# Attention scores from stacked high and low parts: two matmuls over 128 rows in place of three over 64

## The chip, the cores and the metric

The kernel runs on one core of a Trainium2 chip. The metric is the device time of one execution in microseconds (us). Times are given as the median of several executions. One further execution was recorded by the hardware profiler; every duration of a single instruction below comes from it. TensorE is called PE in the profile, VectorE is DVE, ScalarE is ACT, GpSimd is POOL and SyncE is SP.

## What is computed

One layer of a decoder on 512 tokens of width 1024: a SwiGLU feed-forward layer (FFN 1), a mixer, and a second feed-forward layer (FFN 2), each with an RMS norm before and after. The mixer projects the tokens to a pooling part and to an attention part. The attention part has 8 query heads and 2 key/value heads of 64 elements, looks back over 128 tokens and works in blocks of 128 queries. Of the reference, this is what the change touches:

```python
def swa_with_sinks(q, k, v, sinks):
    ...
    kb = jnp.concatenate([kp[:, :-1], kp[:, 1:]], axis=2)
    vb = jnp.concatenate([vp[:, :-1], vp[:, 1:]], axis=2)
    s = jnp.einsum('bnqkgd,bnjkd->bnkgqj', qb, kb,
                   preferred_element_type=jnp.float32) * (HEAD_DIM ** -0.5)
    ...
    s = jnp.where(valid[None, :, None, None], s, NEG_INF)
    ...
    p = jax.nn.softmax(jnp.concatenate([s, sink], axis=-1), axis=-1)[..., :-1]
    o = jnp.einsum('bnkgqj,bnjkd->bnqkgd', p.astype(v.dtype), vb)
    return o.reshape(B, S, ATTN_WIDTH)
```

## The kernel before

All products are made from split numbers. A float32 operand is written as a high part (a cast to the type fp32r, made by ACT) and a low part (the operand less its high part, made by DVE or POOL), and `mm3` (lines 363 to 368) adds three matmuls: high by high, high by low, low by high. In the profile the three are lines L366, L367 and L368.

The work comes in three stages. `gate_up` and `down_proj` do FFN 1 up to about 350 us of the span. The mixer runs between about 350 and 490 us. FFN 2 fills the rest. The mixer is not a stage of its own in the code: `gate_up("f2", ...)` calls `last_steps` ahead of its first block, and that calls `mixer()` and `output()`. Since `gate_up` makes its first four blocks inside `in_order()` (line 521), the instructions of PE, DVE, ACT and POOL in all of the mixer stand on their engines in the order in which the code writes them.

`mixer()` (lines 1169 to 1260) is that order, written out by hand. The four token tiles t = 0 to 3 (128 tokens each) pass through these steps, which are interleaved with one another and with the pooling part:

- `qkv_block(t)` projects the tile to q, k and v on PE; `qkv_out(t)` copies the result to the tile `z` (ACT, L966 to L971) and rotates a part of it (POOL, L977 to L981).
- `turn(t)` transposes k (one transpose, bank `tk`) and q (four, bank `tq`) on PE (L988, L990), so that the 64 elements of head group v lie on partitions 64v to 64v+63. Then ACT copies the high part of k (L991) and of q (L994) out of the banks, each over all 128 partitions at once, and DVE subtracts (L992, L995) for the low parts.
- `scores(t)` makes the scores of the 8 heads, in four PSUM banks of two heads. A head takes the three matmuls of `mm3` on the 64 partitions of its group; the stationary operand is q (64x128), the moving one is k: 256 keys, or 128 for t = 0. That makes 24 matmuls for a tile.
- `tops(t)` adds the mask to the scores and takes the maxima (DVE, L1025), then makes the negated maximum `nm` (L1033) and `es` (L1035). `exps(t, half)` takes the exponentials on ACT (L1041, L1046), four heads in each half. `normalise(t)` divides: the sum on DVE (L1052, L1053), four heads on DVE (L1056) and four on ACT (L1058).
- `turn_probs(t, v)` transposes the probabilities on PE (L1067, bank `pt`) and splits them on ACT (L1071, `ph`) and DVE (L1072, `pl`). `values(t, v)` multiplies them by v on PE and copies the result on ACT (L1083, `o`).
- `pool_in`, `pool_sums`, `pool_mid` and `pool_out` are the pooling part. Its projection (tile `pu`) is the PE work that `run(g)` puts between the attention steps; its sums run on POOL. `pool_out` reads its bank `py` twice on ACT (L1150, L1152) and once on DVE (L1153).
- `W.more(n)` splits n weight tiles ahead of their use: the high part on ACT (L166); the low part (L172) on POOL within `qkv_block` 2 and 3, on DVE elsewhere.

PSUM has 8 banks in one pool. The 24 tiles of 128x512 in the pool `h` are shared by keys, queries, probabilities and the rest; a tile takes a slot at its first write and gives it back after its last reader.

Of the kernel before, what the change touches and what calls it, by code (L numbers as in the profile page):

```python
# [10 lines left out]
F32 = mybir.dt.float32  # L11
BF16 = mybir.dt.bfloat16
F32R = mybir.dt.float32r
I32 = mybir.dt.int32
AF = mybir.ActivationFunctionType
ALU = mybir.AluOpType
# [3 lines left out]
P = 128  # L20
# [6 lines left out]
HD = 64  # L27
NH = 8
NKV = 2
# [38 lines left out]
def trunk_layer(  # L68
# [4 lines left out]
    nc = tc.nc  # L73
# [32 lines left out]
    def in_order():  # L106
        return tc.manual_schedule(engines={E.PE, E.DVE, E.Activation, E.Pool})

    def bank(name):
        return banks_of["pool"].tile([P, 512], F32, tag="ps", name=name)  # L110
# [4 lines left out]
    def slot(name, shape=(P, 512), dtype=F32):  # L115
        return slots_of["pool"].tile(list(shape), dtype, tag="h", name=name)
# [188 lines left out]
    rows = wk.tile([12, P], F32, tag="sqs", bufs=2, name="rows")  # L305
# [57 lines left out]
    def mm3(ps, wl, xr, first, last, open_=False):  # L363

        (wh, wlo), (xh, xlo) = wl, xr
        nc.tensor.matmul(ps, wh, xh, start=first, stop=False, skip_group_check=open_)  # L366
        nc.tensor.matmul(ps, wh, xlo, start=False, stop=False, skip_group_check=open_)  # L367
        nc.tensor.matmul(ps, wlo, xh, start=False, stop=last, skip_group_check=open_)  # L368

    def act_pair(name, shape=(P, 2, S)):  # L370
        hi = ap.tile(list(shape), F32R, tag="ahi", name=f"{name}_hi")
        lo = ap.tile(list(shape), F32R, tag="alo", name=f"{name}_lo")
        return hi, lo
# [7 lines left out]
    def scaled(t, r, g, name, between=lambda: None, xn=None):  # L381
        xn = xn or [slot(f"xn_{name}{t}{n}") for n in range(2)]
        for n in range(2):
            at = slice(n * 512, (n + 1) * 512)
            nc.vector.scalar_tensor_tensor(xn[n], xs[t][:, at], r, g[n], ALU.mult, ALU.mult)
            if n == 0:
                between()
        return xn
# [474 lines left out]
    at = 0  # L863
# [53 lines left out]
    def size1(t):  # L917
        sizes1[t] = sizes(t, "b")

    def root1(t):  # L920
        roots1[t] = power(mean_square(sizes1[t], EPS, f"b{t}"), f"b{t}")

    def norm1(t):
        xn = ap.tile([P, 2, 512], F32, tag=("ahi", "alo")[t % 2], name=f"xn_b{t}")
        xns[t] = scaled(t, roots1[t], g3, "b", xn=[xn[:, n] for n in range(2)])

    def turn1(t):
        if t == 0:
            xT2.extend(act_pair(f"xT2_{i}") for i in range(4))
        transposes(t, xns[t], xT2, "mx")  # L930
# [16 lines left out]
            w = W.get(f"{nm}{k // per}", 0)  # L947
            mm3(ps, (xh[at], xl[at]), (w[0][:, k % per], w[1][:, k % per]), k == 0, k == KD - 1)

    kTh, kTl = slot("kTh", dtype=F32R), slot("kTl", dtype=F32R)  # L950
    vh, vl = slot("vh", (P, NT, P), F32R), slot("vl", (P, NT, P), F32R)
    zs, qT, scored, probs, ra, ds, outs = {}, {}, {}, {}, {}, {}, {}
    osq = {}

    def qkv_block(t, between):
        pq = bank(f"pq{t}")
        project(pq, t, "wq", 2)
        between()
        pkv = bank(f"pkv{t}")
        project(pkv[:, :256], t, "wkv", 4)  # L960
        z = big(f"z{t}", (P, 768))
        zs[t] = (z, pq, pkv)

    def qkv_out(t):
        z, pq, pkv = zs[t]
        nc.scalar.mul(  # L966
            z[:, :512].rearrange("p (j v d) -> p v j d", v=NKV, d=HD),
            pq.rearrange("p (v j d) -> p v j d", v=NKV, d=HD), HD**-0.5,
        )
        nc.scalar.copy(z[:, 512:], pkv[:, :256])  # L970
        nc.scalar.copy(vh[:, t], z[:, 640:])  # L971
        rot = z[:, :640].rearrange("p (h d) -> p h d", d=HD)[:, :, :ROT]
        rot = rot.rearrange("p h (a f) -> p h a f", a=2)
        RS = [P, NH + NKV, 2, 8]
        a = wk.tile(RS, F32, tag="ra", bufs=1, name=f"ra{t}")
        b = wk.tile(RS, F32, tag="rb", bufs=1, name=f"rb{t}")
        nc.gpsimd.tensor_tensor(a, rot, cosT[:, t, None, None, :].to_broadcast(RS), ALU.mult)  # L977
        nc.gpsimd.tensor_tensor(b, rot, sinT[:, t, None, None, :].to_broadcast(RS), ALU.mult)
        nc.gpsimd.tensor_tensor(rot[:, :, 0], a[:, :, 0], b[:, :, 1], ALU.subtract)
        nc.gpsimd.tensor_tensor(rot[:, :, 1], a[:, :, 1], b[:, :, 0], ALU.add)  # L980
        nc.gpsimd.tensor_tensor(vl[:, t], z[:, 640:], vh[:, t].bitcast(F32), ALU.subtract)  # L981

    def turn(t):

        z, _, _ = zs.pop(t)
        pk, pq = bank(f"tk{t}"), bank(f"tq{t}")
        at = slice(t * P, (t + 1) * P)
        nc.tensor.transpose(pk[:, :P], z[:, 512:640], ident)  # L988
        for j in range(4):
            nc.tensor.transpose(pq[:, j * P : (j + 1) * P], z[:, j * P : (j + 1) * P], ident)  # L990
        nc.scalar.copy(kTh[:, at], pk[:, :P])  # L991
        nc.vector.tensor_tensor(kTl[:, at], pk[:, :P], kTh[:, at].bitcast(F32), ALU.subtract)  # L992
        qh, ql = slot(f"qh{t}", dtype=F32R), slot(f"ql{t}", dtype=F32R)
        nc.scalar.copy(qh, pq)  # L994
        nc.vector.tensor_tensor(ql, pq, qh.bitcast(F32), ALU.subtract)  # L995
        qT[t] = (qh, ql)

    def scores(t):
        qh, ql = qT.pop(t)
        nk = 256 if t else 128  # L1000
        k0 = (t - 1) * P if t else 0
        banks = []
        for v in range(NKV):
            rows = slice(HD * v, HD * (v + 1))
            ka = (rows, slice(k0, k0 + nk))
            for i in range(2):
                ps = bank(f"s{t}{v}{i}")
                for j in range(2):
                    qa = (rows, slice((2 * i + j) * P, (2 * i + j + 1) * P))
                    mm3(ps[:, j * 256 : j * 256 + nk], (qh[qa], ql[qa]), (kTh[ka], kTl[ka]), True, True)  # L1010
                banks.append(ps)
        scored[t] = (banks, nk)

# [152 lines left out]
    def run(g):  # L1166
        next(pi[g])

    def mixer():
        with in_order():  # L1170
            root1(2)
            W.more(1)
            norm1(2)
            qkv_block(0, lambda: None)
            qkv_out(0)
            add_to_x(3)
            size1(3)
            root1(3)
            norm1(3)
        nc.scalar.copy(wph, wpr)  # L1180
        nc.gpsimd.tensor_tensor(wpl, wpr, wph.bitcast(F32), ALU.subtract)
        pcols = bank("pcols")
        nc.tensor.transpose(pcols[:, :12], rows, ident[:12, :12])
        nc.vector.tensor_copy(cols, pcols[:, :12])
        nc.vector.tensor_tensor(cols[:, 4:8], cols[:, 0:4], cols[:, 4:8], ALU.mult)
        qkv_block(1, lambda: turn1(2))
        turn1(3)
        qkv_out(1)
        turn(0)
        W.run_ahead = 2  # L1190
        W.lo = nc.gpsimd
        qkv_block(2, lambda: (scores(0), tops(0), turn(1), exps(0, 0), exps(0, 1)))
        qkv_out(2)
        normalise(0)
        qkv_block(3, lambda: (W.more(2), scores(1), tops(1), turn(2), exps(1, 0)))
        W.more(2)
        turn_probs(0, 0)
        turn_probs(0, 1)
        exps(1, 1)
        qkv_out(3)  # L1200
        run(3)
        normalise(1)
        scores(2)
        run(3)
        tops(2)
        pool_sums(3)
        values(0, 0)
        values(0, 1)
        turn(3)
        exps(2, 0)  # L1210

        turn_probs(1, 0)
        attn_out(0)
        run(2)
        scores(3)
        exps(2, 1)
        tops(3, (0,))
        values(1, 0)
        turn_probs(1, 1)
        normalise(2)  # L1220
        tops(3, (1,))
        run(2)
        values(1, 1)
        pool_sums(2)
        W.lo = nc.vector

        turn_probs(2, 0)
        attn_out(1)
        exps(3, 0)
        pool_mid(3)  # L1230
        run(1)
        W.more(1)
        attn_rms(0)
        values(2, 0)
        turn_probs(2, 1)
        exps(3, 1)
        normalise(3)
        run(1)
        pool_sums(1)
        yT[0:2] = [act_pair(f"yT{i}") for i in (0, 1)]  # L1240
        pool_out(3, True)
        values(2, 1)

        turn_probs(3, 0)
        attn_rms(1)
        attn_out(2)
        W.more(1)
        pool_mid(2)
        run(0)
        values(3, 0)  # L1250
        turn_probs(3, 1)
        run(0)
        pool_sums(0)
        W.more(2)
        pool_out(2)
        values(3, 1)
        pool_mid(1)
        pool_mid(0)
        attn_rms(2)
        attn_out(3)  # L1260
# [163 lines left out]
```

## Time and profile before

| what | us |
| --- | --- |
| median of 3 executions | 831.22 |
| lowest and highest | 830.76, 831.99 |
| the profiled execution, its own time | 830.7 |
| its span in the profile | 828.9 |
| PE busy | 816.6 (99%) |
| DVE busy | 661.2 (80%) |
| ACT busy | 468.1 (56%) |
| POOL busy | 209.2 (25%) |

The span is the time between the first and the last instruction of the profile; 1.8 us of the profiled execution lie around it. An engine's busy time is the union of its instructions. Matmuls are pipelined, so that a matmul's own duration is longer than its distance to the next one: for PE the distance between two starts is what a matmul costs. A row of the timeline gives the start, the duration, the engine, the source line, the operation, output and inputs, and the shapes; in brackets stands how long the engine had been idle and what it had waited for.

### The profile page before, as it was taken

What the parts mean: (1) busy time and instruction counts of PE and PEld (TensorE: products, weight loads), DVE (VectorE), ACT (ScalarE), POOL (GpSimd) and SP (SyncE); (2) the same over time, 40 slices, a digit from 0 to 9 for tenths busy, and PEclk for the clock granted to TensorE, in tenths of its full rate; (3) what the DMA queues carried; (4) which work ended last, traced back from release to release, by engine and by line L of the source; (5) the groups of instructions that cost most, each with busy time, mean ns of one, the idle gap of its engine ahead of it and who ended that gap; (6) DMA issues with size and microseconds to landing.
All of it is one profiled execution on the core that took longest, in us unless ns stands there. A gap on an engine that the chain in (4) does not pass through costs nothing.

```text
span 828.9 us, 14054 instructions
## 1 busy us (share of the span) xinstructions
PE 816.6 (99%) x5521; PEld 749.8 (90%) x5521; DVE 661.2 (80%) x859; ACT 468.1 (56%) x743; POOL 209.2 (25%) x289
## 2 busy tenths in 40 slices
PE   9999999999999999999999999999999999999996
PEld 6999999999998888888878889999999999988885
DVE  7997787777989987955766789877877778799875
ACT  6554444444556666737887476544444445566661
POOL 3113344433310000244532020133344333200001
PEclk9999999999999999999999999999999999999999
DMA  9248889988895666511005410388888888966622
GB/s 319 72 127 229 229 229 230 233 238 238 240 279 201 201 226 191 166 52 52 26 26 153 152 51 28 115 237 229 232 229 230 229 233 238 264 220 212 211 84 101
DMA packets 96592, 150.25 MB, mean 181 GB/s; under 512 B 6918, under 2 KB 53646, under 8 KB 96527
## 3 DMA queue, kind: packets, MB, share of 16 engines
q1 hardware_dynamic: 76812, 103.22, 38.5%
q0 software_dynamic: 19712, 46.15, 23.7%
q8 instruction: 43, 0.70, 0.3%
q14 instruction: 23, 0.18, 0.1%
q10 hardware_dynamic: 2, 0.00, 0.0%
HBM read 147.25 MB, written 48.23 MB: 236 GB/s over the span
## 4 chain that ended last, share of the span: by engine, by line
PE 87%; DVE 7%; ACT 4%; issue 2%; POOL 1%; DVEq 0%; POOLq 0%; ACTq 0%
PE f_x L366 13%; PE f_x L367 13%; PE f_x L368 13%; PE f_y L366 7%; PE f_y L368 7%; PE f_y L367 7%; PE f_z L367 4%; PE f_z L368 4%; PE f_z L366 4%; PE f_c L483 1%; PE f_c L482 1%; PE f_c L485 1%; PE tr_f L431 1%; PE pq L366 1%; PE pq L367 1%
## 5 line engine op out<-in xcount | busy, mean ns | idle before, releaser
L172 DVE TENSOR_TENSOR f_d_lo<-f_d_raw,f_d_hi 128x1024 fp32r<-128x1024 f32 x84 | 94.8, 1132 | 23.5 <-ACT f_d_hi L166 23.5
L574 POOL DMA_DIRECT2D f_t<-in_ffn_w_down x132 | 89.5, 752 | 83.4 <-issue 51.6
L166 ACT CAST f_d_hi<-f_d_raw 128x1024 fp32r<-128x1024 f32 x84 | 79.6, 976 | 25.2 <-PE f_z L368 10.7
L600 ACT COPY f_h<-f_y 128x512 f32<-128x512 f32 x20 | 11.7, 587 | 75.7 <-PE f_y L368 75.7
L571 POOL COPY f_k<-f_h 1x1 f32<-1x1 f32 x18 | 21.0, 1166 | 125.9 <-DVE f_h L563 125.9
L609 ACT ACTIVATE f_s<-f_s 128x1024 f32<-128x1024 f32 x20 | 21.2, 1061 | 41.5 <-DVE f_s L608 41.5
L574 POOL DMA_DIRECT2D f_t<-f_t x44 | 32.1, 800 | 37.7 <-issue 30.2
L606 ACT COPY f_s<-f_x 128x512 f32<-128x512 f32 x20 | 11.7, 587 | 42.4 <-PE f_x L368 42.4
L366 PE MATMUL f_x<-f_d_hi,f1e_hi 128*128 128x512 f32 x88 | 34.4, 391 | 0.0
L367 PE MATMUL f_x<-f_d_lo,f1e_hi 128*128 128x512 f32 x88 | 34.3, 389 | 0.0
L368 PE MATMUL f_x<-f_d_hi,f1e_lo 128*128 128x512 f32 x88 | 34.2, 389 | 0.0
L366 PE MATMUL f_x<-f_d_hi,f2e_hi 128*128 128x512 f32 x88 | 34.2, 389 | 0.0
L367 PE MATMUL f_x<-f_d_lo,f2e_hi 128*128 128x512 f32 x88 | 34.2, 389 | 0.0
L368 PE MATMUL f_x<-f_d_hi,f2e_lo 128*128 128x512 f32 x88 | 34.2, 389 | 0.0
L643 ACT CAST f2e_hi<-f_h 128x1024 fp32r<-128x1024 f32 (+1 forms) x21 | 20.5, 979 | 20.8 <-DVE f_h L635 4.9
L590 ACT COPY f_s<-f_x 128x512 f32<-128x512 f32 x20 | 11.7, 586 | 36.2 <-PE f_x L368 29.8
L643 ACT CAST f1e_hi<-f_h 128x1024 fp32r<-128x1024 f32 (+1 forms) x21 | 20.5, 980 | 20.6 <-DVE f_h L637 4.9
L341 POOL TENSOR_TENSOR r_f1po<-ms_f1po,half 128x1 f32<-128x1 f32 x4 | 2.5, 628 | 105.3 <-DVE ms_f1po L346 105.3
L341 POOL TENSOR_TENSOR r_f2po<-ms_f2po,half 128x1 f32<-128x1 f32 x4 | 2.5, 627 | 103.7 <-DVE ms_f2po L346 103.7
L366 PE MATMUL po<-wo_hi,yT_hi 128*128 128x512 f32 x64 | 25.3, 395 | 0.0
L644 DVE TENSOR_TENSOR f2e_lo<-f_h,f2e_hi 128x1024 fp32r<-128x1024 f32 (+1 forms) x21 | 23.6, 1132 | 2.1 <-ACT f2e_hi L643 2.1
L644 DVE TENSOR_TENSOR f1e_lo<-f_h,f1e_hi 128x1024 fp32r<-128x1024 f32 (+1 forms) x21 | 23.6, 1131 | 2.1 <-ACT f1e_hi L643 2.1
(1030 smaller groups left out, 3411.8 us busy)
## 6 DMA issues: line engine op xcount, KB each, us to landing
f_t<-in_ffn_w_down POOLq DMA_DIRECT2D x132, 256.0 KB, 6.2
f_d_raw<-f_t SPq DMA_DIRECT2D x40, 512.0 KB, 4.0
f_d_raw<-in_ffn_w_down SPq DMA_DIRECT2D x30, 512.0 KB, 4.3
f_t<-f_t POOLq DMA_DIRECT2D x44, 256.0 KB, 6.6
f_raw<-in_ffn_w_gu SPq DMA_DIRECT2D x8, 512.0 KB, 5.6
x<-in_x SPq DMA_DIRECT2D x4, 512.0 KB, 4.0
f_d_raw<-f_t SPq DMA_DIRECT2D x8, 256.0 KB, 3.4
wq_raw<-in_w_in SPq DMA_DIRECT2D x4, 512.0 KB, 3.6
```

Of the source, the lines that this page charges most:

```text
L166: nc.scalar.copy(hi, src)
L172: return lambda: engine.tensor_tensor(lo, src, hi.bitcast(F32), ALU.subtract)
L366: nc.tensor.matmul(ps, wh, xh, start=first, stop=False, skip_group_check=open_)
L367: nc.tensor.matmul(ps, wh, xlo, start=False, stop=False, skip_group_check=open_)
L368: nc.tensor.matmul(ps, wlo, xh, start=False, stop=last, skip_group_check=open_)
L571: then = nc.gpsimd.tensor_copy(tick, hs[(c - 1) // 4][:1, 0, (c - 1) % 4, :1]).ins
L574: nc.gpsimd.dma_start(to, part, accum_op=op, max_dma_last_dim=2048)
L590: on_act.append(nc.scalar.copy(sg[:, :, a], px[:, :, a]).ins)
L600: on_act.append(nc.scalar.copy(h[1], py[:, :, a]).ins)
L609: on_act.append(nc.scalar.activation(sg, sg, AF.Silu, scale=-1.0).ins)
L643: nc.scalar.copy(hi, src)
L644: nc.vector.tensor_tensor(lo, src, hi.bitcast(F32), ALU.subtract)
```

## The change

Keys and queries are kept in another form. For each head group v there is now a tile `kTh[v]` that holds the high parts of k twice, on the group's own 64 partitions and on the other 64, and a tile `kTl[v]` with the low parts on the own partitions and zeros on the others. The query tile `qs[v]` holds the high parts of q on the own partitions and the low parts on the others. A head's scores are then two matmuls over all 128 partitions: `qs` by `kTl` is high by low, and `qs` by `kTh` is high by high plus low by high. That is 16 matmuls for a tile in place of 24.

`turn(t)` makes the parts for one group at a time: for k one ACT copy, one DVE copy (from the same 64 PSUM partitions to the other 64 of SBUF) and one DVE subtraction for each group, for q one ACT copy and one DVE subtraction for each group. That is four ACT and six DVE instructions where there were two and two. POOL writes the zeros once, after the norm of the last tile. The keys take four slots of the pool `h` in place of two.

```diff
-    kTh, kTl = slot("kTh", dtype=F32R), slot("kTl", dtype=F32R)
+    kTh = [slot(f"kTh{v}", dtype=F32R) for v in range(NKV)]
+    kTl = [slot(f"kTl{v}", dtype=F32R) for v in range(NKV)]
+    own = [slice(HD * v, HD * (v + 1)) for v in range(NKV)]
...
     def turn(t):
...
-        nc.scalar.copy(kTh[:, at], pk[:, :P])
-        nc.vector.tensor_tensor(kTl[:, at], pk[:, :P], kTh[:, at].bitcast(F32), ALU.subtract)
-        qh, ql = slot(f"qh{t}", dtype=F32R), slot(f"ql{t}", dtype=F32R)
-        nc.scalar.copy(qh, pq)
-        nc.vector.tensor_tensor(ql, pq, qh.bitcast(F32), ALU.subtract)
-        qT[t] = (qh, ql)
+        qs = [slot(f"q{v}{t}", dtype=F32R) for v in range(NKV)]
+        for v in range(NKV):
+            nc.scalar.copy(kTh[v][own[v], at], pk[own[v], :P])
+            nc.vector.tensor_copy(kTh[v][own[1 - v], at], pk[own[v], :P])
+            nc.vector.tensor_tensor(
+                kTl[v][own[v], at], pk[own[v], :P], kTh[v][own[v], at].bitcast(F32), ALU.subtract
+            )
+        for v in range(NKV):
+            nc.scalar.copy(qs[v][own[v]], pq[own[v]])
+            nc.vector.tensor_tensor(
+                qs[v][own[1 - v]], pq[own[v]], qs[v][own[v]].bitcast(F32), ALU.subtract
+            )
+        qT[t] = qs

     def scores(t):
-        qh, ql = qT.pop(t)
+        qs = qT.pop(t)
         nk = 256 if t else 128
         k0 = (t - 1) * P if t else 0
         banks = []
+        keys = slice(k0, k0 + nk)
         for v in range(NKV):
-            rows = slice(HD * v, HD * (v + 1))
-            ka = (rows, slice(k0, k0 + nk))
             for i in range(2):
                 ps = bank(f"s{t}{v}{i}")
                 for j in range(2):
-                    qa = (rows, slice((2 * i + j) * P, (2 * i + j + 1) * P))
-                    mm3(ps[:, j * 256 : j * 256 + nk], (qh[qa], ql[qa]), (kTh[ka], kTl[ka]), True, True)
+                    to = ps[:, j * 256 : j * 256 + nk]
+                    at = slice((2 * i + j) * P, (2 * i + j + 1) * P)
+                    nc.tensor.matmul(to, qs[v][:, at], kTl[v][:, keys], start=True, stop=False)
+                    nc.tensor.matmul(to, qs[v][:, at], kTh[v][:, keys], start=False, stop=True)
                 banks.append(ps)
...
             norm1(3)
+            for v in range(NKV):
+                nc.gpsimd.memset(kTl[v][own[1 - v]].bitcast(F32), 0.0)
```

## The prediction, made before the result was known

> **What bounds the kernel now.** I read the page first, then the chain of work in order of time through the mixer, then the waits of PE and ACT there, then the timeline around `turn` and `scores`.
>
> ```profile
> span 828.9 us, 14054 instructions
> PE 87%; DVE 7%; ACT 4%; issue 2%; POOL 1%; DVEq 0%; POOLq 0%; ACTq 0%
> ```
>
> Over the whole span PE carries the chain (87%). That is an average, and the change works in one stage only, so the chain in order of time has to say who carries it there:
>
> ```profile
> 414.01 0.59 ACT o L1083
> ...
> 431.11 0.70 DVE pl L1072
> 431.86 0.44 PE o L367
> ```
>
> From the first projections of the mixer up to 414.01 the chain is PE, matmul after matmul. Then it goes over to ACT and DVE, and comes back to PE at 431.86. So PE's pace up to 414 is not what the mixer's end hangs on. Two stretches of the table of busy times show the same (columns: PE, PEld, DVE, ACT, POOL, clock, DMA):
>
> ```profile
> 388.00:414.00 26.00, 26.00 (x162) 21.41 (x161) 17.84 (x59) 22.25 (x64) 12.71 (x17) 1.00 0.13 40
> 414.00:426.50 12.50, 11.54 (x64) 9.00 (x62) 9.16 (x23) 11.39 (x33) 4.40 (x8) 1.00 0.12 42
> ```
>
> ACT is busy 22.25 of 26 us and then 11.39 of 12.5, and it works strictly in the written order. What it waited for in the mixer, and PE's only wait that matters there:
>
> ```profile
> PE pt L1067 <- DVE st L1056: 1.0, 1, 1.0
> ...
> ACT kTh L991 <- PE tk L988: 8.2, 2, 6.2
> ...
> ACT es L1041 <- DVE es L1035: 1.1, 1, 1.1
> ACT o L1083 <- PE o L368: 0.8, 2, 0.5
> ...
> ACT u L1123 <- PE pu L368: 0.4, 1, 0.4
> ```
>
> PE already waits 1.0 us for probabilities (the last `pt`): a faster PE waits there longer. Of ACT's idle time after 389 only 0.8 and 0.4 us were PE's doing. Before that ACT has spare time: 6.2 us ahead of `turn(1)`, 2.0 us ahead of `turn(2)`, 1.1 us ahead of `es` of tile 1.
>
> **PE: 24 matmuls become 16.** Starts of matmuls, in the projection of k and v, the first and last of `scores(0)`, and `scores(2)`:
>
> ```profile
> 361.61 0.87 PE tr_mx L394 x8
> ...
> 372.19 0.32 PE L366 MATMUL s<-kTh,qh 64*128 64x128 f32 x1
> ...
> 374.63 0.33 PE L988 MATMUL tk<-ident,z 128*128 128x128 f32 x1
> ...
> 375.59 0.28 PE L366 MATMUL pkv<-wkv_hi,xT_hi 128*128 128x256 f32 x1
> 375.71 0.28 PE L367 MATMUL pkv<-wkv_lo,xT_hi 128*128 128x256 f32 x1
> ...
> 392.98 0.39 PE L367 MATMUL pu<-xT_lo,wu_hi 128*128 128x512 f32 x1
> 393.21 0.39 PE L368 MATMUL pu<-xT_hi,wu_lo 128*128 128x512 f32 x1
> 393.53 0.38 PE L366 MATMUL s<-kTh,qh 64*128 64x256 f32 x1
> ...
> 396.21 0.50 PE L366 MATMUL pu<-xT_hi,wu_hi 128*128 128x512 f32 x1
> ```
>
> A matmul over 128 rows with 256 columns costs 0.12 us (375.59 to 375.71). `scores(2)` costs 2.68 us from its first start to the next step, for 24 matmuls; 16 times 0.12 is 1.92, so 0.76 us is saved, and three tiles save 2.3. For tile 0 the row of eight 128-column steps gives 0.11 us each: 2.44 less 16 times 0.11 (1.76) is 0.7. The sum is 3.0 us. It may be somewhat more: the first 64-row matmul starts 0.32 after the step ahead of it, where the step ahead cost 0.23 (392.98 to 393.21), so that 0.1 us goes at each change between 64 and 128 rows, and it may go on the way back too: up to 0.2 us for a tile, 3.8 in all. That is the most that the change can bring; it is worked out for PE alone.
>
> **`turn`: two and two instructions become four and six.** Here is `turn(0)`, with both engines free, and one ACT group on 64 partitions:
>
> ```profile
> 368.03 0.26 ACT L991 CAST kTh<-tk 128x128 fp32r<-128x128 f32 x1
> 368.19 0.59 ACT L994 CAST qh<-tq 128x512 fp32r<-128x512 f32 x1
> 368.32 0.29 DVE L992 TENSOR_TENSOR kTl<-tk,kTh 128x128 fp32r<-128x128 f32 x1 [0.40 <-ACT kTh L991]
> 368.81 0.69 DVE L995 TENSOR_TENSOR ql<-tq,qh 128x512 fp32r<-128x512 f32 x1 [0.20 <-ACT qh L994]
> ...
> L1083 ACT COPY o<-o 64x512 f32<-64x512 f32 x6 | 3.5, 579 | 1.0 <-PE o L368 0.8
> ```
>
> A copy of 64x512 takes 0.58 us and one of 128x512 0.59: half the partitions save nothing. So each half costs what the whole did. The hop from ACT to DVE is 0.03 us (368.29 to 368.32). A DVE copy from a bank to the other 64 partitions is not in the trace; it can hardly be over the 0.29 of the subtraction with as many columns, nor under a third of it (0.1), and I take 0.2, midway between the two.
>
> The question on which everything hangs is whether the halves can run beside each other. Both groups of k lie in one PSUM bank, both of q in another. These rows of `pool_out` show how readers of one bank are ordered:
>
> ```profile
> 428.07 0.69 ACT L1150 ACTIVATE yT_hi<-py,cols 128x512 fp32r<-128x512 f32 x1
> ...
> 428.65 0.68 ACT L1152 ACTIVATE sqp<-py,cols 128x512 f32<-128x512 f32 x1
> ...
> 429.37 0.75 DVE L1153 SCALAR_TENSOR_TENSOR yT_lo<-py,cols,yT_hi 128x512 fp32r<-128x512 f32 x1 [2.29 <-ACT sqp L1152]
> ```
>
> DVE L1153 needs `py` and `yT_hi`, and these were there at 428.76. It started at 429.37, 0.04 us after the ACT instruction that merely reads the same bank ahead of it. So reads of one bank by two engines are kept in the written order. If that holds for the other 64 partitions of the bank as well, then the ACT copy of group 1 waits for the DVE instructions of group 0, in k and in q, and ACT's queue stands still behind it. The chain from the moment DVE is free is then: copy and subtraction of k (0.49), hop, ACT copy (0.29 with the hop), hop, copy and subtraction (0.49 and 0.03), `ql` of group 0 (0.69, less 0.08 for issue ahead), hop and the second `qs` (0.62). That is 2.5 us until ACT is free again, and 0.7 more until the second `ql`. The row before had ACT free 0.75 us after its first copy, and not dependent on DVE at all.
>
> **Along the four tiles, with such waits.** `turn(0)`: the whole takes 3.5 us from 368.03, to 371.6, and `scores(0)` starts at 372.19. Hidden, with 0.6 us to spare.
>
> ```profile
> 375.54 0.17 DVE L1033 TENSOR_SCALAR nm<-m 128x8 f32<-128x8 f32 x1
> ...
> 376.04 1.28 ACT L1041 ACT_TABLE_LOAD   x1
> ...
> 386.23 2.39 POOL L172 TENSOR_TENSOR wu_lo<-wu_raw,wu_hi 128x1024 fp32r<-128x1024 f32 x1
> ...
> 388.03 0.62 DVE L1033 TENSOR_SCALAR nm<-m 128x8 f32<-128x8 f32 x1
> 388.69 0.17 DVE L1035 TENSOR_TENSOR es<-snk,nm 128x8 f32<-128x8 f32 x1
> ...
> 388.89 0.21 ACT L1041 ACTIVATE es<-es 128x8 f32<-128x8 f32 x1 [1.15 <-DVE es L1035]
> ...
> 402.29 0.17 DVE L1035 TENSOR_TENSOR es<-snk,nm 128x8 f32<-128x8 f32 x1
> ...
> 402.49 0.21 ACT L1041 ACTIVATE es<-es 128x8 f32<-128x8 f32 x1
> ```
>
> `turn(1)`: DVE is free of tile 0's `nm` and `es` at about 375.8, some 0.3 earlier with four matmuls in a bank for six. 375.5 plus 2.5 is 378.0, when the exponentials' table load can start: 2.0 us later than 376.04. The exponentials, `z` of tile 2 and the weight casts behind them on ACT move by 2.0. The idle 2.0 ahead of `turn(2)` takes this up on ACT; the two POOL subtractions (the second one at 386.23) still start 2.0 later.
>
> `turn(2)`: the DVE instruction `nm` took 0.62 us at 388.03 where it took 0.17 at 375.54; it ended at 388.65, with POOL's subtraction (386.23 + 2.39 = 388.62). DVE was held by POOL. With POOL 2.0 later its first subtraction ends at about 388.2, `nm` gets through there, and DVE comes to the keys at about 388.5. ACT is free 2.5 us later, at 391.0, and only then makes `es` and the exponentials of tile 1, which began at 388.89: 2.1 us late, and with them everything on ACT and DVE up to `es` of tile 2.
>
> `turn(3)`: there ACT's `es` (402.49) follows DVE's (402.29 + 0.17) at once. With the wait between them it comes 2.5 us later still: 4.6 us late. From there to 414 ACT gets back the 0.8 us that it had waited for PE's `o`. The 0.4 before `u` is lost in the wait that follows. 4.6 - 0.8 = 3.8, and so late are the probabilities of tile 3 for which PE waits. PE, 3 us early, waits 1.0 + 3.0 + 3.8 in all; behind it the chain is PE's again (431.86), and what comes late there stays late.
>
> **Edits that I cost at nothing.** The two fills with zeros stand on POOL between the last tile's root and the split of the pooling weights, which is not needed before the pooling product behind the last `run(1)`; without that cover the price would be their own time. The two further slots: keys die with `scores(3)`, when I count all 24 slots taken, none missing; a missing slot would hold the mask step of tile 3 to the end of `scores(3)`, under 1 us, inside a wait that is there anyway. A transposed bank is held 2 us longer; PE takes it again later than that.
>
> **Forecast: 3.8 us slower.** 830.7 + 3.8 = 834.5 for the profiled execution. The median of the runs is 0.5 above that execution, so 831.2 + 3.8 = 835.0.
>
> **The rivals.**
>
> 1. *The halves run side by side (not slower).* The trace has no case of two engines on different partitions of one bank, so it does not decide. The Trainium skill, page "PSUM — Partial Sum Buffer", section "PSUM bank collisions raise a hardware error", states that engines collide in a bank only within a quadrant of 32 partitions, and calls guarding by bank "the simple version". By that rule group 1 need not wait for group 0. No run here shows it yet. The time then: `turn(1)` ends on ACT 0.2 earlier (0.7 from PE, less 0.5 for the second `qs`), so POOL and with it `nm` and `es` come 0.2 earlier; the added ACT work of `turn(2)` lies in the idle 1.1 before `es`, that of `turn(3)` is taken from the 0.4 before `u` and from DVE's lead; then the 0.8 of `o` is gained. Together 1.0 faster: 831.2 - 1.0 = 830.2. Were `nm` not held by POOL, the start of tile 1's maxima, 1.1 earlier (0.7 from tile 0, 0.4 from four matmuls for six in its first bank and no change of rows), would count in full and another 0.9 be gained: 829.3.
> 2. *PE decides after all.* All of PE's 3.0 us arrive: 831.2 - 3.0 = 828.2. Against it speak ACT's 22.25 of 26 us and the chain at 414.01; for it only the average of the page.
> 3. *Slower still.* `es` may be held as `nm` was. The Trainium skill, page "SBUF — State Buffer", section "Who interferes with whom", states that a DVE instruction with two SBUF inputs contends with a POOL instruction that reads SBUF, and that the loser is blocked to the end; `nm`'s 0.62 us agrees with such a hold. `es` has two inputs in SBUF. If POOL's second subtraction goes in ahead of it, DVE comes to the keys some 2.2 us later (2.39 less 0.17): 6.0 slower, 831.2 + 6.0 = 837.2. It decides where the second subtraction starts within the 0.2 us between `nm` and `es`.
>
> That the change does not do what it says is no rival here: the 16 matmuls are plain in the code.
>
> **How the numbers follow.** The forecast case with waits for the bank has half of the chance: 0.33 as worked out and 0.17 with rival 3. Rival 1 has 0.35, of which 0.1 is with `nm` free or with other gains past the bound. Rival 2 has 0.08. The other 0.07 are waits of about half the size (in k or in q alone), around 1 slower. What a measurement can tell from no change is 0.2%, or 1.7 us. Faster by more: 0.1 + 0.08 and a little of rival 1, 0.22. Within: the rest of rival 1 and the half sizes, 0.28. Slower: 0.50. The two signs hold most of the chance, so the range goes from rival 1 with `nm` free (829.3, taken to 829.0) to rival 3 (837.2, taken to 837.4). The likeliest case's own range is 833.5 to 836.5, from the copy's bounds (0.1 to 0.29, four copies on the path of tiles 2 and 3) and up to 1 us of waits that overlap.
>
> **What would show it.** Right: ACT idle before the second `kTh` and the second `qs` of a tile, released by DVE L-lines of `turn`; `es` of tile 2 some 4 to 5 us after 402.49; PE's wait at `pt` of several us. Wrong: both `qs` copies within 1.2 us of each other on ACT with no idle time between; then rival 1. If PE's wait at `pt` has gone and its 3 us are at the end, rival 2. If `scores` does not shrink to about 1.9 us, the first step is wrong.

## The result: 7.7 us slower, and the profile after

| what | us |
| --- | --- |
| before, median of 4 executions beside it | 830.99 |
| after, median of 4 executions | 838.7 (838.07 to 839.11) |
| ratio, with its 95% interval | 1.0091 [1.0078, 1.0103] |
| the profiled execution of after, its own time | 838.97 |
| its span | 837.1 (before 828.9) |

Slower had been forecast, by 3.8 us; it is 7.7, and the time lies above the range. The page of the changed kernel, its span and its chain by engine:

```profile
span 837.1 us, 14019 instructions
...
PE 81%; DVE 9%; ACT 6%; issue 2%; POOL 1%; DVEq 0%; POOLq 0%; ACTq 0%
```

PE carries 81% of the chain where it carried 87%; DVE and ACT have taken over most of the difference. The stage shows in the table of busy times (columns as in the prediction: PE, PEld, DVE, ACT, POOL, clock, DMA):

```profile
388.00:414.00 26.00, 21.04 (x110) 17.03 (x108) 16.73 (x40) 17.71 (x49) 15.23 (x18) 0.87 0.14 40
414.00:426.50 12.50, 11.90 (x63) 9.14 (x64) 10.59 (x36) 11.20 (x32) 2.33 (x4) 1.00 0.01 2
```

In the first stretch every engine but POOL does less than before: PE 21.04 us for 26.00, DVE 16.73 for 17.84, ACT 17.71 for 22.25. Nobody is the bound there: they wait for each other. For what, the list of waits between 360 and 440 us says (engine and line, whom it waited for, us in total, times, the longest):

```profile
ACT kTh L997 <- DVE kTl L999: 7.7, 4, 4.4
...
PE s L1021 <- DVE pl L1084: 3.9, 1, 3.9
...
ACT q L1003 <- DVE q L1004: 3.1, 4, 0.8
...
PE pt L1079 <- DVE st L1068: 1.0, 1, 1.0
```

ACT now waits for DVE at the second copy of k and the second copy of q of each tile, four times each, 10.8 us in all. These are the waits on readers of one bank that the forecast rests on. The timeline of `turn(2)`, DVE, ACT and POOL together, in order of start:

```profile
386.43 4.75 POOL L172 TENSOR_TENSOR wu_lo<-wu_raw,wu_hi 128x1024 fp32r<-128x1024 f32 x2
...
387.17 0.26 ACT L997 CAST kTh<-tk 64x128 fp32r<-64x128 f32 x1
...
387.71 1.16 DVE L1045 TENSOR_SCALAR nm<-m 128x8 f32<-128x8 f32 x1
388.90 2.31 DVE L1047 TENSOR_TENSOR es<-snk,nm 128x8 f32<-128x8 f32 x1
391.22 0.28 DVE L998 CAST kTh<-tk 64x128 fp32r<-64x128 f32 x1
391.52 0.28 DVE L999 TENSOR_TENSOR kTl<-tk,kTh 64x128 fp32r<-64x128 f32 x1
391.84 0.26 ACT L997 CAST kTh<-tk 64x128 fp32r<-64x128 f32 x1 [4.42 <-DVE kTl L999]
392.12 0.58 ACT L1003 CAST q<-tq 64x512 fp32r<-64x512 f32 x1
392.13 0.29 DVE L998 CAST kTh<-tk 64x128 fp32r<-64x128 f32 x1 [0.33 <-ACT kTh L997]
392.44 0.29 DVE L999 TENSOR_TENSOR kTl<-tk,kTh 64x128 fp32r<-64x128 f32 x1
392.76 0.68 DVE L1004 TENSOR_TENSOR q<-tq,q 64x512 fp32r<-64x512 f32 x1
393.48 0.58 ACT L1003 CAST q<-tq 64x512 fp32r<-64x512 f32 x1 [0.78 <-DVE q L1004]
394.09 0.21 ACT L1053 ACTIVATE es<-es 128x8 f32<-128x8 f32 x1
```

Two things are to be read here. First the chain: DVE is free at 391.22 and ACT at 394.06, 2.84 us later, in steps that change engines three times (DVE, ACT, DVE, ACT). Second, DVE came to the keys so late because `nm` took 1.16 us and `es` 2.31, where 0.17 each is their price when POOL is quiet (375.54 and 375.75 of before). `nm` ended at 388.87 and `es` at 391.21; POOL's two subtractions ended at about 388.8 (half of 4.75 behind 386.43) and at 391.18. The `es` on ACT is 5.2 us later than before (394.09 for 388.89). Then, from the same timeline, tile 2 and the end:

```profile
407.33 1.04 POOL L1141 TENSOR_TENSOR win<-win 128x510 f32<-128x510 f32 x1
407.37 1.02 DVE L1045 TENSOR_SCALAR nm<-m 128x8 f32<-128x8 f32 x1
...
408.43 0.17 DVE L1047 TENSOR_TENSOR es<-snk,nm 128x8 f32<-128x8 f32 x1
...
411.47 0.21 ACT L1053 ACTIVATE es<-es 128x8 f32<-128x8 f32 x1
...
434.71 1.46 PE L1079 MATMUL pt<-ident,st 128*128 128x128 f32 x8 [1.04 <-DVE st L1068]
...
440.14 0.44 PE L367 MATMUL o<-pl,vh 128*64 128x512 f32 x1
```

The rows of before that belong beside these, where the prediction does not show them already:

```profile
401.17 1.04 POOL L1129 TENSOR_TENSOR win<-win 128x510 f32<-128x510 f32 x1
...
402.08 0.17 DVE L1033 TENSOR_SCALAR nm<-m 128x8 f32<-128x8 f32 x1
...
426.44 1.46 PE L1067 MATMUL pt<-ident,st 128*128 128x128 f32 x8 [0.96 <-DVE st L1056]
```

DVE's `es` of tile 2 is 6.1 us late (408.43 for 402.29), ACT's 9.0 (411.47 for 402.49), the last probabilities 8.3 (434.71 for 426.44), and the return to PE 8.3 (440.14 for 431.86). That is the whole of the span's 8.2.

### The profile page after: what moved, and what is told of

The parts are those of the page before. It is cut to its first block, busy times and chain, and to the rows that moved or that the text cites. A ratio compares the mean times of both kernels' runs of the same rounds, so it can differ in the third digit from the quotient of the medians.

```text
span 837.1 us, 14019 instructions
## 1 busy us (share of the span) xinstructions
PE 818.0 (98%) x5489; PEld 749.9 (90%) x5489; DVE 671.0 (80%) x875; ACT 471.9 (56%) x751; POOL 209.8 (25%) x291
## 4 chain that ended last, share of the span: by engine, by line
PE 81%; DVE 9%; ACT 6%; issue 2%; POOL 1%; DVEq 0%; POOLq 0%; ACTq 0%
PE f_x L366 13%; PE f_x L367 13%; PE f_x L368 13%; PE f_y L368 7%; PE f_y L367 7%; PE f_y L366 7%; PE f_z L368 4%; PE f_z L367 4%; PE f_z L366 4%; ACT st L1058 2%; PE f_c L483 1%; PE f_c L482 1%; PE f_c L485 1%; DVE st L1037 1%; PE tr_f L431 1%
```

## The experiments

Theory: reads of one PSUM bank by ACT and DVE are kept in the written order, across the halves of the partitions too, and that is the loss. Rivals: the added instructions themselves (two more on ACT and four more on DVE for each tile) are the loss; the matmuls over 128 rows cost more than they save; and, for the size, a further wait that the forecast does not have. The first four kernels ran on the same chip, beside a before of 830.74 (27 executions).

**The four ACT copies first.** The same ten instructions in another order, with nothing added and nothing left out:

```diff
         for v in range(NKV):
             nc.scalar.copy(kTh[v][own[v], at], pk[own[v], :P])
+        for v in range(NKV):
+            nc.scalar.copy(qs[v][own[v]], pq[own[v]])
+        for v in range(NKV):
             nc.vector.tensor_copy(kTh[v][own[1 - v], at], pk[own[v], :P])
...
         for v in range(NKV):
-            nc.scalar.copy(qs[v][own[v]], pq[own[v]])
             nc.vector.tensor_tensor(
                 qs[v][own[1 - v]], pq[own[v]], qs[v][own[v]].bitcast(F32), ALU.subtract
```

> The changed kernel with the ten instructions of turn in another order: the four ACT copies first, then the six DVE instructions. Nothing is added or left out, only no ACT copy is written behind a DVE reader of its bank. Theory (the 7.7 us come from ACT copies that are held behind DVE readers of the same PSUM bank): ACT shows no idle time between the four copies of a tile, es of tile 1 is not late, the last wait of PE at pt is back at about 426 us of the span or up to 1.5 us earlier, and the time is 829.5 to 831.5 us. Rival A (the added work itself costs it: four and six instructions for two and two): still 835 us or more. Rival B (PE's 3 us arrive once the waits are gone): 828 us.

Measured: 830.46, ratio 0.9994 [0.9985, 1.0003]. Each set against the before beside it, that is 8.0 less than the changed kernel (0.3 under before for 7.7 over). ACT's waits at `turn` and at `es`, from the list of waits of this version:

```profile
ACT kTh L997 <- PE tk L992: 4.6, 2, 4.4
ACT es L1055 <- DVE es L1049: 2.8, 2, 2.3
```

And the rows of `turn(2)` in its timeline, ACT's and DVE's:

```profile
385.68 0.53 ACT L997 CAST kTh<-tk 64x128 fp32r<-64x128 f32 x2 [0.19 <-PE tk L992]
386.23 1.17 ACT L999 CAST q<-tq 64x512 fp32r<-64x512 f32 x2
...
387.49 1.98 DVE L1047 TENSOR_SCALAR nm<-m 128x8 f32<-128x8 f32 x1
...
389.70 0.21 ACT L1055 ACTIVATE es<-es 128x8 f32<-128x8 f32 x1 [2.29 <-DVE es L1049]
```

The copies run back to back and ACT waits for no reader on DVE. So the written order of the readers cost the 8 us, and not the instructions. But `nm` is held here too (1.98), and ACT waits for it: the `es` of tile 1 is 0.8 us late (389.70 for 388.89) and so are the last probabilities (427.20 for 426.44), where the expectation had both on time. The time itself lies in the expected stretch.

**The alternating halves alone.** The kernel before, its scores unchanged, with `turn` done in halves:

```diff
-        nc.scalar.copy(kTh[:, at], pk[:, :P])
-        nc.vector.tensor_tensor(kTl[:, at], pk[:, :P], kTh[:, at].bitcast(F32), ALU.subtract)
+        own = [slice(HD * v, HD * (v + 1)) for v in range(NKV)]
+        for v in range(NKV):
+            nc.scalar.copy(kTh[own[v], at], pk[own[v], :P])
+            nc.vector.tensor_tensor(kTl[own[v], at], pk[own[v], :P], kTh[own[v], at].bitcast(F32), ALU.subtract)
```

and the same for q.

> The kernel before with one part of the change alone: the scores keep their three matmuls over 64 rows and the keys and queries their tiles, but turn makes the halves one after the other in the changed order (ACT, DVE, ACT, DVE for k and again for q). Theory: nearly all of the loss comes back without any of the new matmuls; a tile's chain is shorter by the two copies of k (0.6 us), so 836 to 838 us. Rival A (added work, not waits): 0.6 us of ACT and 0.9 us of DVE for each tile, of which two tiles lie on the path, so 831.5 to 833 us.

Measured: 838.81, ratio 1.0094 [1.0080, 1.0108]. From its list of waits:

```profile
ACT kTh L993 <- DVE kTl L994: 5.6, 4, 4.0
...
PE s L366 <- DVE pl L1075: 3.5, 1, 3.5
ACT qh L997 <- DVE ql L998: 3.0, 4, 0.7
```

The alternation makes the loss by itself, without the stacked scores and without DVE's extra copies. The time is above the expected stretch; in this kernel, too, `es` of tile 1 took 2.30 us on DVE. The changed kernel, which has PE's gain and DVE's copies of k besides, is within 0.4 us of this one (7.7 over before for 8.1), so PE's gain does not make up for the waits; how much of it is left beside those copies cannot be read from this.

**PE's part alone.** The kernel before, its `turn` unchanged, with two 128-row matmuls for three of 64. It leaves out the separation of the two head groups: each matmul sums over both, so the scores are not those of the layer, and only the time of this kernel counts:

```diff
-                    qa = (rows, slice((2 * i + j) * P, (2 * i + j + 1) * P))
-                    mm3(ps[:, j * 256 : j * 256 + nk], (qh[qa], ql[qa]), (kTh[ka], kTl[ka]), True, True)
+                    qa = (slice(None), slice((2 * i + j) * P, (2 * i + j + 1) * P))
+                    kk = (slice(None), slice(k0, k0 + nk))
+                    to = ps[:, j * 256 : j * 256 + nk]
+                    nc.tensor.matmul(to, qh[qa], kTl[kk], start=True, stop=False)
+                    nc.tensor.matmul(to, ql[qa], kTh[kk], start=False, stop=True)
```

> The kernel before with the other part alone: turn and its tiles as before, but each head's scores are two matmuls over all 128 rows of the tiles as they are. That mixes the two head groups in the scores; the work of PE is that of the change, 16 matmuls for 24. Theory (ACT and DVE set the mixer's pace): of PE's 3.0 to 3.8 us at most 1 to 2 arrive, 829 to 830.5 us, and PE's wait at the last pt grows by the rest. Rival B: 827 to 828 us.

Measured: 829.29, ratio 0.9981 [0.9972, 0.9990]: 1.5 us of PE's 3.0 arrive. PE's wait at the last `pt` was expected to grow and did not; it is 1.0 us as before. Where the rest may stay, its list of waits says:

```profile
ACT es L1044 <- DVE es L1038: 3.6, 2, 2.1
```

and, behind that, its timeline of DVE:

```profile
387.37 1.07 DVE L1036 TENSOR_SCALAR nm<-m 128x8 f32<-128x8 f32 x1
...
401.89 0.85 DVE L1036 TENSOR_SCALAR nm<-m 128x8 f32<-128x8 f32 x1
```

`nm` of tile 1 comes 0.66 us earlier than before and is held 0.45 longer; that of tile 2 is held 0.68 where it was not held. That these holds are what keeps the rest back is argued here; the kernels without them, below, test it.

**Two pairs of banks.** The written order of the changed kernel, with k and q transposed twice, into separate banks for the two groups (five more transposes for each tile):

```diff
+        pk2, pq2 = bank(f"tk2{t}"), bank(f"tq2{t}")
+        nc.tensor.transpose(pk2[:, :P], z[:, 512:640], ident)
+        for j in range(4):
+            nc.tensor.transpose(pq2[:, j * P : (j + 1) * P], z[:, j * P : (j + 1) * P], ident)
+        pks, pqs = (pk, pk2), (pq, pq2)
...
-            nc.scalar.copy(kTh[v][own[v], at], pk[own[v], :P])
+            nc.scalar.copy(kTh[v][own[v], at], pks[v][own[v], :P])
```

> The changed kernel with its order of turn kept, but k and q are transposed twice, into a second pair of banks, from which group 1 is read: five more transposes for a tile (0.55 us of PE) and four banks in place of two. Theory (order of readers within one bank): ACT's idle time before the second kTh and the second q of each tile is gone though the written order is the same; the time falls by 4 us or more, to 830 to 834 us, the rest being short of banks. Rival C (what holds ACT is not the bank but the order of instructions on tiles in SBUF, or something else in that order): the waits of ACT on DVE stay and the time is 838 us or more.

Measured: 832.0, ratio 1.0017 [1.0008, 1.0026]. In its list of waits ACT waits in `turn` for PE alone:

```profile
ACT kTh L1002 <- PE tk L992: 5.7, 2, 5.2
...
ACT kTh L1002 <- PE tk L996: 0.6, 2, 0.3
```

With the groups in different banks the same order costs 1.3 us over before in place of 7.7. What this 1.3 is made of was not taken apart: the kernel has five more transposes for a tile, and its `nm` of tile 1 is held too (1.72 us). So the cause is the shared bank, and not the alternation on two engines as such. Each bank is one tile of the program here, so these runs do not tell an order kept for the bank from one kept for the tile.

With that the cause is shown, but not the size: the waits had been forecast, and the loss was twice the forecast. The second question was therefore whether POOL's holds of `nm` and `es` are the missing half. The next four ran beside a before of 831.19 (27 executions).

**POOL's subtraction in pieces.** The changed kernel, with each `wu_lo` as four subtractions of 128x256:

```diff
-            return lambda: engine.tensor_tensor(lo, src, hi.bitcast(F32), ALU.subtract)
+            n = src.shape[-1] // 4 if name.startswith("wu") and engine is nc.gpsimd else src.shape[-1]
+
+            def lows():
+                for c in range(0, src.shape[-1], n):
+                    at = (Ellipsis, slice(c, c + n))
+                    engine.tensor_tensor(lo[at], src[at], hi[at].bitcast(F32), ALU.subtract)
+
+            return lows
```

> The changed kernel, with GpSimd's four subtractions wu_lo (128x1024, 2.39 us each) cut into four of 128x256 each. Theory (nm and es of tile 1 are held to the end of a GpSimd subtraction, which in the changed kernel cost DVE 0.99 and 2.14 us beyond the 0.17 that each takes): no hold is longer than a piece of some 0.7 us, so es of tile 1 on DVE ends 1.5 to 2.5 us earlier against the start of its maxima, the last matmul before the mixer's end comes 1.5 to 2.5 earlier, and the time goes from 838.7 to 836.2 to 837.2. The waits of ACT on DVE's readers of the same bank (2.85 us for a tile) stay. Rival (the 2.31 us of es were a wait on something else that the trace does not name, and the excess over the forecast is the readers' chain alone): es still takes 1 us or more and the time stays at 838.4 to 839.0.

Measured: 835.9, ratio 1.0057 [1.0044, 1.0069], just under the expected stretch. POOL and DVE in its timeline around `turn(2)` (the row of POOL is eight pieces in a row):

```profile
386.38 5.61 POOL L177 TENSOR_TENSOR wu_lo<-wu_raw,wu_hi 128x256 fp32r<-128x256 f32 x8
...
387.65 0.20 DVE L1052 TENSOR_SCALAR nm<-m 128x8 f32<-128x8 f32 x1
387.89 0.66 DVE L1054 TENSOR_TENSOR es<-snk,nm 128x8 f32<-128x8 f32 x1
```

and ACT in its list of waits:

```profile
ACT kTh L1004 <- DVE kTl L1006: 5.0, 4, 1.8
...
ACT q L1010 <- DVE q L1011: 3.1, 4, 0.8
```

No hold is longer than a piece (5.61 / 8 = 0.70). `nm` and `es` took 0.86 together, 2.61 less than the 3.47 of the changed kernel, and `nm` of tile 2, which then came at another moment of POOL's work, took 0.25 for 1.02. Of the loss against before 3.0 us went (4.7 for 7.7). The waits for q are unchanged.

**Both together, the control, and an order by groups.** The pieces with the ACT copies first; the pieces in the kernel before; and the first of these with DVE's six instructions ordered by group (k's two, then q's one, for group 0 and then for group 1).

> The four ACT copies of a tile ahead of its six DVE instructions, and GpSimd's wu_lo subtractions in four pieces. With the waits on the banks gone, the reordered kernel took 830.5 and its nm of tile 1 still took 1.98 us. Theory (that hold was on the path, since es of tile 1 on ACT waited 2.3 us for DVE): 1 to 1.8 us come off, 828.7 to 829.5. Rival (ACT's own work has taken the path over, the hold lies beside it): 830.1 to 830.7.

> The kernel before, with GpSimd's wu_lo subtractions in four pieces and nothing else: what the pieces are worth by themselves. nm of tile 1 took 0.62 us there in place of 0.17, so at most 0.45 us can come off: 830.3 to 830.9. If the pieces cost POOL's start-up on the path of the weights, it would be slower than before by up to 1 us.

> As the version with the four ACT copies first and the pieces, with DVE's six instructions of a tile ordered by head group: copy and subtraction of k, then q's subtraction of group 0, then the same of group 1. The scores of group 0 need only the first three, so PE's wait of 1.1 us ahead of scores (for q's low part) should shrink by 0.3 to 0.6. If PE's pace counts there, 0.2 to 0.5 us faster than that version; if ACT and DVE set the pace as the chain says, the same within 0.2 us.

Measured: 830.69, ratio 0.9995 [0.9986, 1.0004]; 831.61, ratio 1.0007 [0.9998, 1.0015]; 830.68, ratio 0.9995 [0.9986, 1.0005]. None can be told from before. The expected gain of the first one was a miss, and so was that of the control. The third came out the same as the first. It had been meant to shorten PE's wait of 1.1 us for q ahead of the scores; that wait stands in the list of the version without pieces, and in neither of these two, so there was nothing to shorten. `nm` and `es` of tile 1 in the timeline of the first, with the ACT copies first and the pieces:

```profile
387.33 0.72 DVE L1054 TENSOR_SCALAR nm<-m 128x8 f32<-128x8 f32 x1
388.08 0.66 DVE L1056 TENSOR_TENSOR es<-snk,nm 128x8 f32<-128x8 f32 x1
```

and in that of the second, the kernel before with the pieces:

```profile
388.35 0.79 DVE L1040 TENSOR_SCALAR nm<-m 128x8 f32<-128x8 f32 x1
389.17 0.66 DVE L1042 TENSOR_TENSOR es<-snk,nm 128x8 f32<-128x8 f32 x1
```

Both instructions are held by a piece each, 1.38 and 1.45 us together. In the kernel before, where only `nm` had been held (0.62 and 0.17), that is a loss, and its `es` of tile 2 is now held as well (1.05). With the ACT copies first it is 0.77 less than the 2.15 without pieces (1.98 and 0.17), and the last probabilities come 0.8 earlier (426.41 for 427.20); why the time does not show that is open. Pieces make a hold shorter and leave it in place.

**`nm` on ACT.** So the last step takes both out of POOL's reach: ACT makes `nm`, and DVE makes `es` after the keys and queries of the next tile.

```diff
 def tops(t, parts=(0, 1)):
...
-        nc.vector.tensor_scalar(nm, m, -1.0, None, ALU.mult)
         es = sm.tile([P, NH], F32, tag="es", bufs=2, name=f"es{t}")
-        nc.vector.tensor_tensor(es, snk, nm, ALU.add)
...
 def exps(t, half):
         if half == 0:
...
-            nc.scalar.activation(es, es, AF.Exp)
...
+            nc.scalar.mul(nm, m, -1.0)
+            nc.vector.tensor_tensor(es, snk, nm, ALU.add)
...
+        if half == 1:
+            nc.scalar.activation(es, es, AF.Exp)
```

It was put into the version with the ACT copies first, into the kernel before and into the changed kernel, beside a before of 830.83 (16 executions).

> The version with the four ACT copies first, with nm (the negated maxima) made by ACT ahead of the exponentials, and DVE's es put behind the keys and queries of the next tile, its exponential ahead of the second half. GpSimd can then hold nothing between the maxima and the exponentials. The chain of the version without this had nm of tile 1 with 1.99 us and nm of tile 2 with 0.75 on it, each with 0.18 of es behind; an ACT nm costs some 0.3. Theory (these holds are on the path, and eat the change's gain on PE): 1 to 2 us come off 830.5, 828.5 to 829.5. Rival (the path goes beside them, as the pieces of GpSimd's work, which gave no measurable gain there, could mean): 830.1 to 830.8.

> The kernel before with the same move of nm and es alone: the control. Its nm of tile 1 took 0.62 us and ACT waited 1.1 for es; its es of tile 2 followed at once. 0.3 to 0.8 us come off: 830.2 to 830.7. If it gains as much as the version with the changed scores does, the gain there is the move's and not the change's.

> The changed kernel, its order of ACT and DVE in the turn kept, with the same move of nm and es. DVE comes to the keys of tile 2 some 3.3 us earlier (nm 1.16 and es 2.31 stood ahead of them, less the 0.17 which each took free of GpSimd), and to those of tile 3 0.9 earlier. Theory (the excess over the forecast was these holds): 838.7 less 3.5 to 4.5, 834.2 to 835.2, and ACT still waits some 2 us or more for DVE's readers in each of tiles 2 and 3. Rival (what is left of 838.7 is readers' waits alone, and the pieces had already taken all that there was): 835.6 to 836.2.

Measured: 828.24, ratio 0.9968 [0.9956, 0.9980], just under the expected stretch; 830.80, ratio 1.0001 [0.9992, 1.0010], no gain where 0.3 to 0.8 had been expected; 834.86, ratio 1.0044 [1.0031, 1.0057], as expected. From the timeline of the first, PE and ACT:

```profile
382.81 0.28 PE L1023 MATMUL s<-kTl,q 128*128 128x256 f32 x1
...
384.72 0.27 PE L992 MATMUL tk<-ident,z 128*128 128x128 f32 x1
...
386.84 0.21 ACT L1053 ACTIVATE nm<-m 128x8 f32<-128x8 f32 x1
...
424.55 1.46 PE L1082 MATMUL pt<-ident,st 128*128 128x128 f32 x8 [1.14 <-DVE st L1071]
```

and from the list of waits of the third:

```profile
ACT kTh L997 <- DVE kTl L999: 4.4, 4, 1.7
ACT q L1003 <- DVE q L1004: 3.1, 4, 0.8
```

The loss of the changed kernel falls from 7.7 us to 4.0 when `nm` and `es` are out of reach; the readers' waits stay. The first and the third kernel differ in nothing but the order of the readers: it costs 6.6 us (834.86 for 828.24). With the readers reordered as well, `nm` of tile 1 is made at 386.84 and the last probabilities come at 424.55 (before 426.44). That version beats both kernels, by 0.32% against before. Against the control, which gains nothing, it is 2.6 us faster: that is the change's own gain with its readers in a good order, nearly all of PE's 3.0.

## Why the prediction was right in kind and short by half

- **PE, 24 to 16 matmuls: right.** In the last version of the study, the one that beats both, the 16 matmuls of `scores(1)` take from 382.81 to 384.72, 1.91 us for the forecast 1.92.
- **The readers of one bank: right, 0.34 short.** The chain from DVE free to ACT free was forecast at 2.5 us and took 2.84 in `turn(2)`. The copy from the bank to the other partitions took 0.28 in place of 0.2, and each half of k needs 0.62 from the copy's start to ACT (391.22 to 391.84) in place of 0.49 and a hop. At `turn(1)` the table load was 2.3 late for 2.0 (378.38 for 376.04).
- **The rival that the halves run side by side: wrong for this kernel.** That its 830.2 is about what the reordered version took (830.46) is luck: in that version `nm` was held 1.98 us, longer than the rival had it. The Trainium skill, page "PSUM — Partial Sum Buffer", section "PSUM bank collisions raise a hardware error", states that two engines collide only within a bank and a quadrant of 32 partitions, and that a guard by bank is the simple version. The waits here go by bank, over different quadrants as well (4.42 us, in the row of 391.84); that they vanish with a second bank agrees. Whether the chip itself would bear the halves side by side in one bank was not tried.
- **`turn(2)`, the step that failed.** The prediction let `nm` through at 388.2 and then took `es` at its free price, so that DVE came to the keys at 388.5. It came at 391.22: `nm` was held to 388.87, because POOL started 2.5 us late and not 2.0, and `es` was then held by POOL's second subtraction. That is rival 3, which had 0.17. It is the mis-sized term: 2.7 us. The Trainium skill, page "SBUF — State Buffer", section "Who interferes with whom", states that the one that issues first has the shared ports for its whole instruction. The pieces agree: the hold went from 2.31 to 0.66 when POOL's instruction went from 2.39 to 0.70.
- **`turn(3)`: a hold that was not foreseen.** `nm` of tile 2 took 1.02 in place of 0.17, under a pooling sum on POOL (407.33 to 408.37); in before that sum was all but over (402.21) when `nm` came (402.08). Being late moved DVE's small steps under other POOL work: 0.85.
- **The sum.** 3.8 forecast, and 2.7 (`es` and `nm` of tile 1), 0.85 (`nm` of tile 2) and 0.34 twice (the chains) make 8.0 of the 8.3 by which the last probabilities were late. The 0.8 that was to be regained was regained to 0.7 (9.0 at ACT's `es`, 8.3 at the end).
- **"ACT, not PE, sets the pace": wrong for the part of the mixer where it matters.** The prediction saw that the chain is PE, matmul after matmul, up to 414.01, and concluded that PE's pace up to there does not count. That reading is the wrong way round: a chain that runs through PE's matmuls moves when they are fewer. The prediction let a faster PE only wait longer. But the work of ACT and DVE on a tile starts at PE's scores, and these came earlier. 1.5 us arrived with PE's part alone, and 2.6 when POOL's holds were out of the way too (828.24, where rival 2 had all of the 3.0). The busy share of ACT (22.25 of 26 us) did not show that; ACT still waited.
- **Edits at nothing.** `turn(0)` and the fills with zeros were hidden. The banks were not: PE waited 3.9 us in `scores(2)` for a bank of `pt` that DVE emptied late. PE's waiting so lies there and not, as forecast, at the last `pt`, where the wait is 1.0 as before; the chain of the changed kernel runs on ACT and DVE then, so this wait is PE's own.

## What to carry to other kernels

When a copy is cut in halves, write all of one engine's reads of a bank ahead of the other engine's reads, or give each half a bank: the order of ten instructions was worth 8.0 us here (6.6 with POOL's holds out of the way), and the added instructions no more than the 0.4 us by which the gain of 2.6 falls short of PE's estimated 3.0. Before costing a delay, look at what the delayed small instructions will then lie beside: a step of 0.17 us on DVE cost up to 2.31 beside POOL. A gain on an engine that seems to have slack may be stopped only by such a hold; take it away and measure the gain with a control.

## What the runs showed of the hardware

A small instruction of 128x8 on DVE (`nm` or `es`) that came while a subtraction or a pooling sum of POOL was running took as long as that still ran: 0.66 us beside pieces of 0.70, up to 2.31 beside 2.39. Each DVE instruction can be held anew: two in a row were held by two pieces in a row (0.72 and 0.66). DVE's copies of k out of PSUM kept their 0.28 us beside POOL's pieces (the first at 388.56, the pieces from 386.38 to 391.99). The clock granted to PE was 0.87 from 388 to 414 us in the changed kernel, where PE had a gap of 3.9 us, and 0.93 in the version in pieces, where the gap was 2.1 us; it was 1.00 in the kernel before. In the changed kernel the loss lies behind the gap: from 399 to 402 us the clock was 0.50, and matmuls of 512 columns started 0.43 us apart (400.55 and 400.98) in place of 0.23. The length of the gap alone does not decide it. PE waited 1.14 us for the last probabilities both in the reordered version with `nm` on ACT and in the changed kernel with `nm` on ACT; from 414 to 440 us the clock was 1.00 in the first and 0.93 in the second. That a gap lowers the clock was not tried by itself.
